# First norm of a hybrid S5 and conformer trunk: statistics asked for a block ahead, slabs loaded before the large S5 arrays, first block modulated like the others

## The chip, the cores and the metric

One core of one Trainium2 chip runs the whole program. The metric is the device time of one execution, in microseconds (us). All tensors are float32. The core has five engines that run their own instruction streams in order: TensorE (PE, the matmuls), VectorE (DVE), ScalarE (ACT), GpSimd (POOL) and SyncE (SP, which here only issues DMAs).

## The reference, cut to what matters

One trunk layer over 2048 latent tokens of width 1024, with 256 context tokens in front:

```python
mod_l = silu(c) @ ada_w + ada_b            # shift, scale, gate: 6 x 1024
mod_c = silu(c_ctx) @ ada_w + ada_b
nl = rmsnorm(x,   norm1_g) * (1 + sc1)  + sh1       # (2048, 1024)
nc = rmsnorm(ctx, norm1_g) * (1 + csc1) + csh1      # (256, 1024)
zl = nl @ w_in                             # columns: S5 input 512 | conformer 1024 | gates 2048
zc = nc @ w_in[:, :512]                    # S5 input of the context
ys = s5_mixer(zl[:, :512], zc)             # bidirectional scan, latents start from the context's state
ya = (gelu(ys) * sigmoid(gelu(ys) @ w_glu)) @ w_a
yb = conformer(zl[:, 512:1536]) @ w_b      # GLU, depthwise conv of width 31, LayerNorm, swish
h  = x + g1 * ((sigmoid(ga) * ya + sigmoid(gb) * yb) @ w_out)
h  = h + g2 * conv_ffn(modulate(rmsnorm(h, norm2_g), sh2, sc2))
out = rmsnorm(h, final_g)
```

An rmsnorm needs, for every token, the reciprocal root of its mean square. The kernel holds tokens along the free axis of a tile (channels on partitions), so this number is needed as a row that is the same in all partitions.

## The kernel before, in words

**Products.** Every large product is done in three passes (`mm3`, L462 to L464): both operands are split into a rounded part and a remainder, `hi` and `lo`, and hi by hi, hi by lo and lo by hi are summed in PSUM. The split of a weight chunk is a copy on ACT (L449) and a subtraction on POOL or, later, on DVE (L453).

**Modulation vectors** (`ada_first`). 2048 columns of `ada_w` come in 8 slabs of 1 MB (L574). Each slab feeds four matmuls (L577, 32 in all, two records each in the trace). The four sums are copied to `adarow`, two on DVE and two on ACT (L584), and 16 small transposes (L586) and two DVE operations (L591, L593) turn them into columns `A1` and `S1`. Between the slabs `after(k)` issues other work: pieces of the S5 parameters (`s5_params`, a generator), the statistics of the context and, at the end, of the first token block.

**Statistics** (`half_stats`, 256 tokens each). A load of the tokens (L619), two ACT squares with a running sum (L622), and `rstd`: five small DVE operations and a power on POOL (L476 to L482). `row` then makes the row: for each 128 tokens a diagonal matrix `dg` on DVE (L630) and a matmul with ones (L631), which leaves the row in PSUM.

**First norm.** The latents are worked in 4 blocks of 512 tokens, `nl0` to `nl3`, loaded transposed (L638, tiles `xt`). The context, `nlc`, has 256. The context and block 0 are normed in two steps: `early` multiplies by the row (L644, on DVE, it needs only the statistics) and `late` multiplies by `A1` and adds `S1` (L650), rounds on ACT (L652) and subtracts (L654). Blocks 1 to 3 go through `prepare` and `modulate`: row and `A1` in one DVE operation (L661), shift and rounding in one ACT operation (L662), remainder on DVE (L663).

**S5 input** (`pair`). Column tiles of 128 are done two at a time, each pair 48 matmuls: two pairs for the context (256 columns each matmul) and two for each block (512 columns). The result leaves PSUM by an ACT copy (L668) and two or one stores issued from ACT's queue (L671). Behind these stand the conformer products, whose tiles go through sigmoids on ACT (L840), the S5 tables (`s5_tables`: 32 groups, per group POOL L245, L246 and L249, DVE L247, L248 and L250, ACT L251 to L253, a store L254, three groups in a buffer of the pool `z8`), the S5 operators (`s5_ops`: POOL and DVE products, PE L308 and L318, stores L310 and L312 and later L328 to L330), and the depthwise conv (L795), whose input `caw` is loaded again from memory by SP (L784).

**What sets the order.** The program asks for work in the order of the Python code; a scheduler places each instruction in its engine's stream, with a head start of 300 for what stands in `urgent`. The streams are fixed before the program runs. Buffers come from small pools (`z8` 8, raw weights 3, `t16` 6, PSUM sums 4), so a load stands in its queue until its buffer is free, and all that is behind it in that queue stands too.

Of the kernel before, what the change touches and what calls it, by code (L numbers as in the profile page):

```python
# [19 lines left out]
CTX = 256  # L20
# [5 lines left out]
NCC = CTX // T  # L26
# [83 lines left out]
def s5_params(nc, ins, scr, st, sp, tp, ident, halfpi, psum):  # L110


    v, g_, a = nc.vector, nc.gpsimd, nc.scalar
    dma = nc.sync.dma_start
# [5 lines left out]
    dma(lm, ins["s5s"])  # L120
    lr, li, ldt = (lm[:, i, :] for i in range(3))
    bri = tp(128, 2, G, H)
    dma(bri, ins["s5b"])
    br, bi = bri[:, 0], bri[:, 1]
    cri = sp.big(128, 2, G, H)
    dma(cri, ins["s5c"])
    cr, ci = cri[:, 0], cri[:, 1]
    dn = sp(48, G)
    dma(dn[32:48, :], ins["s5d"])
    yield  # L130

    q, s = exp_parts(nc, tp, ldt, n)
# [4 lines left out]
    q, s = exp_parts(nc, tp, x, n)  # L137
# [11 lines left out]
    th, k, f = (tp(128, n) for nm in ("th", "kk", "f"))  # L149
# [71 lines left out]
    v.tensor_tensor(f8l, f8, f8h, op=OP.subtract)  # L221
    yield

    bbr, bbi = sp.big(128, G, H), sp.big(128, G, H)
    u1 = tp(128, G, H)
    u2 = tp(128, G, H)
# [204 lines left out]
class Net:  # L431
# [165 lines left out]
    def phase1(self):  # L597
        nc, tc, ins, scr, v, a = self.nc, self.tc, self.ins, self.scr, self.v, self.a
        w_in = ins["w_in"]
        with ExitStack() as ctx:  # L600
# [8 lines left out]
            self.consts()  # L609
            st = {}  # L610
            s5a = s5_params(nc, ins, scr, st, sp, tp, self.ident, self.halfpi, psum)
            nl, srow, xt = {}, {}, {}
            rms = small.tile([128, 18], F32, name="rms", bufs=1)

            def half_stats(i):

                x2 = self.z8("x2", [128, 2, D])
                src = ins["x"][256 * i:256 * i + 256, :] if i < 8 else ins["ctx"]
                self.dma(x2, src.rearrange("(j p) d -> p j d", p=128))  # L619
                ss = small.tile([128, 2], F32, name="nt_ss")  # L620
                for j in range(2):
                    a.activation(x2[:, j, :], x2[:, j, :], AF.Square, accum_out=ss[:, j:j + 1])  # L622
                self.rstd(small, ss, 2, 1.0 / D, rms[:, 2 * i:2 * i + 2])

            def row(i, n):

                ps = psum.tile([128, 512], F32, name="ps", tag="ax")
                for j in range(n // 128):
                    dg = small.tile([128, 128], F32, name="dg")
                    v.tensor_scalar(dg, self.ident, rms[:, 2 * i + j:2 * i + j + 1], None, op0=OP.mult)  # L630
                    self.pe.matmul(ps[:, 128 * j:128 * j + 128], self.ones, dg, start=True, stop=True)  # L631
                return ps

            def raw_block(b):

                for q in range(2):
                    t = self.z8("xt", [128, 4, 512])
                    self.dma(t, ins["xt"][b][:, 4 * q:4 * q + 4])  # L638
                    xt[b, q] = t

            def early(x, rs, n):

                for w in x:
                    v.tensor_tensor(w, w, rs[:, None, :].to_broadcast([128, 4, n]), op=OP.mult)  # L644

            def late(x, hi, lo, r):

                for k in range(8):
                    w = x(k)
                    v.tensor_scalar(w, w, self.A1[:, r, k:k + 1], self.S1[:, r, k:k + 1],  # L650
                                    op0=OP.mult, op1=OP.add)
                    a.copy(hi(k), w)  # L652
                    e = self.g if k % 4 == 3 else v
                    e.tensor_tensor(lo(k), w, hi(k).bitcast(F32), op=OP.subtract)  # L654

            def modulate(b):
                nl[b] = self.nl_tiles(b, "nl")
                for k in range(8):
                    hi, lo = nl[b](0, k), nl[b](1, k)
                    w, s1 = xt[b, k // 4][:, k % 4], self.S1[:, 0, k:k + 1]  # L660
                    v.scalar_tensor_tensor(w, w, self.A1[:, 0, k:k + 1], srow[b], op0=OP.mult, op1=OP.mult)  # L661
                    a.activation(hi, w, AF.Identity, bias=s1)  # L662
                    v.scalar_tensor_tensor(lo, w, s1, hi.bitcast(F32), op0=OP.add, op1=OP.subtract)  # L663
# [11 lines left out]
            def pair(ms, n, x, x0s):  # L675

                pss = [psum.tile([128, 512], F32, name="ps", tag="mm") for _ in ms]
                for k in range(8):
                    for ps, m in zip(pss, ms):
                        self.mm3(ps[:, :n], wu[m][k], x(k), k == 0, k == 7)  # L680
                for ps, m in zip(pss, ms):
                    u_out(ps, n, m, x0s)

            def u_block(b):
                for ms in ((0, 1), (2, 3)):
                    pair(ms, 512, lambda k: (nl[b](0, k), nl[b](1, k)), [NCC + 64 * b])

            xc = self.z8("xt", [128, 8, CTX])

            def after(k):  # L690
                if k == 0:
                    next(s5a)
                if k == 1:
                    self.dma(xc, ins["ctxt"])
                    half_stats(8)
                    early([xc[:, 4 * q:4 * q + 4] for q in range(2)], row(8, CTX)[:, :CTX], CTX)
                if k in (2, 3, 4, 5):
                    next(s5a, None)
                if k == 7:
                    for m in range(2):  # L700
                        wu[m] = self.wtile(ring, w_in, 128 * m)
                    raw_block(0)
                    for i in range(2):
                        half_stats(i)
                    early([xt[0, q] for q in range(2)], row(0, 512), 512)

            self.ada_first(psum, after)
            with self.urgent():
                late(lambda k: xc[:, k], lambda k: nlc(0, k), lambda k: nlc(1, k), 1)
            for m in range(2, 4):  # L710
                wu[m] = self.wtile(ring, w_in, 128 * m)
            nl[0] = self.nl_tiles(0, "nl")
            with self.urgent():
                late(lambda k: xt[0, k // 4][:, k % 4], lambda k: nl[0](0, k), lambda k: nl[0](1, k), 0)
            for ms in ((0, 1), (2, 3)):
                pair(ms, CTX, lambda k: (nlc(0, k), nlc(1, k)), [0, NX - NCC])
            self.low = "v"

            def prepare(b):
                raw_block(b)  # L720
                srow[b] = row(2 * b, 512)
                with self.urgent():
                    modulate(b)

            for i in (2, 3):
                half_stats(i)
            prepare(1)
            for i in (4, 5, 6, 7):
                half_stats(i)
            u_block(0)  # L730
            for _ in s5a:
                pass
            idx = sp(128, NX)
# [3 lines left out]
                        allow_small_or_imprecise_dtypes=True)  # L737
            tabs = s5_tables(nc, scr, st, idx, lambda: self.z8("tab", [128, 6 * NX]), self.halfpi)
            for b in range(1, 4):
                if b < 3:  # L740
                    prepare(b + 1)
                u_block(b)
                for _ in range((0, 3, 6, 9)[b]):
                    next(tabs, None)
            self.dma(self.fw, ins["fdw"])
            up.close()
# [665 lines left out]
```

## Time and profile before

| | |
|---|---|
| Time, 3 runs | 2806.5, 2810.7 and 2811.0 us; median 2810.7 us |
| Profiled execution | 2806.18 us, of which the span of the instructions 2804.4 us |
| PE busy | 2711.9 us, 97% of the span, 12044 matmul records |
| DVE, ACT, POOL busy | 1508.0 us (54%), 822.7 us (29%), 459.3 us (16%) |
| Mean granted TensorE clock | 0.984 of full speed |
| Chain that ended last | PE 75%, DVE 9%, DMA 6%, POOL 5%, issue 2%, ACT 2% |

The table is read so: with PE busy for 97% of the span, what is left to gain lies in the stretches in which PE waits, or runs at half its clock. The profile's page in 40 slices shows the first slice of 70 us with PE busy for 7 tenths and a clock of 8 tenths, the lowest of all. The change lies in the first three slices.

### The profile page before, as it was taken

How to read it: one execution, taken by the hardware profiler on the slowest of the kernel's cores; microseconds unless marked ns; L12 is line 12 of the kernel's file. 1: busy time of each engine (PE TensorE's matmuls, PEld its weight loads, DVE VectorE, ACT ScalarE, POOL GpSimd, SP SyncE). 2: the span in 40 equal slices, each digit the busy share in tenths (PEclk: the TensorE clock that was granted, in tenths of full speed). 3: DMA queues.
4: the chain of work that ended last, by engine and by line, in shares of the span. 5: the costliest groups of instructions: out<-in, count | busy, mean ns of one | idle time of the engine just before them, and what ended most of it. 6: DMA issues, size and time to landing. Idle time of an engine off the chain costs nothing.

```text
span 2804.4 us, 32119 instructions
## 1 busy us (share of the span) xinstructions
PE 2711.9 (97%) x12044; PEld 2203.2 (79%) x12044; DVE 1508.0 (54%) x2312; ACT 822.7 (29%) x1446; POOL 459.3 (16%) x504
## 2 busy tenths in 40 slices
PE   7998999999999999999999999999999989999998
PEld 3786878788887777788888888888888878787887
DVE  5867643433316788566855646556465462414154
ACT  2555412121235443243421222212222132212122
POOL 2256477667600000000000000000000000000000
PEclk8999999999999999999999999999999999999999
DMA  8645745354436576533111111111111153323143
GB/s 315 195 142 165 205 138 153 126 177 147 145 102 202 173 206 200 187 131 113 64 46 57 42 49 49 49 53 46 45 57 42 53 179 107 113 71 135 53 143 98
DMA packets 327308, 334.73 MB, mean 119 GB/s; under 512 B 95336, under 2 KB 240360, under 8 KB 324464
## 3 DMA queue, kind: packets, MB, share of 16 engines
q1 hardware_dynamic: 245680, 235.13, 27.2%
q10 hardware_dynamic: 81472, 97.54, 10.0%
q8 instruction: 95, 1.56, 0.2%
q14 instruction: 61, 0.50, 0.1%
HBM read 230.38 MB, written 102.21 MB: 119 GB/s over the span
## 4 chain that ended last, share of the span: by engine, by line
PE 75%; DVE 9%; DMA 6%; POOL 5%; issue 2%; ACT 2%; SPq 0%; ACTq 0%; POOLq 0%; DVEq 0%
PE ps L464 23%; PE ps L462 23%; PE ps L463 23%; DMA sgab<-d_sg 2%; PE ps L795 1%; DVE Hs L408 1%; PE ps L577 1%; PE ps L385 1%; POOL t L395 1%; DVE Hs L410 1%; DMA slab<-in_ada_w_dram 1%; DMA ada<-in_ada_w_dram 1%; POOL t L394 1%; POOL t L361 1%; PE ps L1112 0%
## 5 line engine op out<-in xcount | busy, mean ns | idle before, releaser
L1242 DVE SCALAR_TENSOR_TENSOR acc<-pad,fw,acc 128x1024 f32<-128x1024 f32 x352 | 450.4, 1282 | 238.9 <-ACT acc L1238 229.5
L477 POOL TENSOR_TENSOR rs_y<-rs_v,mhalf 128x1 f32<-128x1 f32 (+1 forms) x41 | 27.4, 668 | 2048.8 <-DVE rs_v L476 2048.8
L462 PE MATMUL ps<-wd,hhl 128*128 128x512 f32 x704 | 275.6, 393 | 13.5 <-ACT hhl L449 7.3
L463 PE MATMUL ps<-wd,hhl 128*128 128x512 f32 x704 | 275.7, 392 | 0.0
L464 PE MATMUL ps<-wd,hhl 128*128 128x512 f32 x704 | 275.3, 392 | 0.1
L408 DVE TENSOR_TENSOR_SCAN Hs<-m,S 64x287 f32<-64x287 f32 x64 | 68.8, 1075 | 240.5 <-POOL S L396 240.1
L453 DVE TENSOR_TENSOR hhl<-hr,hhl 128x512 fp32r<-128x512 f32 (+1 forms) x110 | 63.0, 582 | 244.4 <-ACT hhl L449 244.1
L453 DVE TENSOR_TENSOR w_ch<-w_raw,w_ch 128x512 fp32r<-128x512 f32 x134 | 106.4, 801 | 137.9 <-ACT w_ch L449 137.5
L462 PEld LDWEIGHTS ps<-wd,hhl 128*128 128x128 f32 x704 | 133.2, 189 | 43.3 <-ACT hhl L449 7.9
L449 ACT CAST w_ch<-w_raw 128x512 fp32r<-128x512 f32 x142 | 87.6, 621 | 267.2 <-PE ps L464 167.1
L463 PEld LDWEIGHTS ps<-wd,hhl 128*128 128x128 f32 x704 | 133.2, 189 | 28.6 <-DVE wd L453 1.0
L464 PEld LDWEIGHTS ps<-wd,hhl 128*128 128x128 f32 x704 | 133.1, 189 | 28.5 <-DVE hhl L453 0.8
L449 ACT CAST hhl<-hr 128x512 fp32r<-128x512 f32 (+1 forms) x110 | 57.2, 534 | 264.5 <-PE ps L464 231.3
L463 PE MATMUL ps<-nm2l,w_ch 128*128 128x512 f32 x344 | 133.8, 389 | 0.0
L464 PE MATMUL ps<-nm2h,w_ch 128*128 128x512 f32 x344 | 133.8, 389 | 0.0
L462 PE MATMUL ps<-nm0h,w_ch 128*128 128x512 f32 x344 | 133.8, 389 | 0.0
L463 PE MATMUL ps<-nm0l,w_ch 128*128 128x512 f32 x344 | 133.8, 389 | 0.0
L463 PE MATMUL ps<-nm1l,w_ch 128*128 128x512 f32 x344 | 133.8, 389 | 0.0
L463 PE MATMUL ps<-nm3l,w_ch 128*128 128x512 f32 x344 | 133.8, 389 | 0.0
L464 PE MATMUL ps<-nm0h,w_ch 128*128 128x512 f32 x344 | 133.8, 389 | 0.0
L462 PE MATMUL ps<-nm1h,w_ch 128*128 128x512 f32 x344 | 133.8, 389 | 0.0
L464 PE MATMUL ps<-nm1h,w_ch 128*128 128x512 f32 x344 | 133.8, 389 | 0.0
(370 smaller groups left out, 6354.5 us busy)
## 6 DMA issues: line engine op xcount, KB each, us to landing
w_raw<-in_ffn_w_up_dram SPq DMA_DIRECT2D x88, 256.0 KB
d_hid<-acc ACTq DMA_DIRECT2D x88, 256.0 KB
w_raw<-in_ffn_w_down_dram SPq DMA_DIRECT2D x76, 256.0 KB
grp<-d_rec SPq DMA_DIRECT2D x32, 576.0 KB
hr<-d_hid SPq DMA_DIRECT2D x66, 256.0 KB
d_sg<-sgg ACTq DMA_DIRECT2D x64, 256.0 KB
ada<-in_ada_w_dram SPq DMA_DIRECT2D x64, 256.0 KB
sgab<-d_sg SPq DMA_DIRECT2D x32, 512.0 KB
```

Of the source, the lines that this page charges most:

```text
L361: g_.tensor_tensor(r1, Hl, tb[:, 0:1, LAT].to_broadcast([128, 2, NCL]), op=OP.mult)
L385: nc.tensor.matmul(ps[:, :NX], sm[:, i, :], ug, start=True, stop=True)
L394: g_.tensor_tensor(t1, S, tb[:, 0:1, :].to_broadcast([128, 2, NX]), op=OP.mult)
L395: g_.tensor_tensor(t2, S[:, ::-1, :], tb[:, 1:2, :].to_broadcast([128, 2, NX]), op=OP.mult)
L408: v.tensor_tensor_scan(Hs[0:64, i, 1:1 + nsc], mb[0:64], S[0:64, i, 0:nsc], 0.0, op0=OP.mult, op1=OP.add)
L410: v.tensor_tensor_scan(Hs[64:128, i, NX - 1 - nsc:NX - 1][:, ::-1], mb[64:128], S[64:128, i, NX - nsc:NX][:, ::-1], 0.0, op0=OP.mult, op1= ...
L449: self.a.copy(hi, src)
L453: e.tensor_tensor(lo, src, hi.bitcast(F32), op=OP.subtract)
L462: mm(ps, wh, xh, start=first, stop=False)
L463: mm(ps, wh, xl, start=False, stop=False)
L464: mm(ps, wl, xh, start=False, stop=last)
L1242: v.scalar_tensor_tensor(acc[:, h], win(h, t // 3, t % 3), fw[:, i, t:t + 1], acc[:, h], op0=OP.mult, op1=OP.add)
```

## The change

The order of loading changes: in `s5_params` the three loads of the larger S5 arrays (`s5b`, `s5c`, `s5d`) stand behind the parameter work instead of before the second slab. In `after` the context is loaded and its statistics are made behind slab 5 instead of slab 1, its row and its `early` step at slab 7, the S5 pieces at 2, 3, 4 and 6 instead of 2 to 5, and at slab 7 block 0's statistics stand ahead of its transposed load. Block 0 loses `early` and `late` and goes through `prepare(0)`. `prepare(b)` asks for block b's row and modulation and then for the loads and statistics of block b+1; it stands between the two column pairs of the block before. Tables are asked for after each pair, 27 of 32 ahead of the conformer products instead of 18.

```diff
@@ s5_params
     bri = tp(128, 2, G, H)
-    dma(bri, ins["s5b"])
...
     cri = sp.big(128, 2, G, H)
-    dma(cri, ins["s5c"])
...
     dn = sp(48, G)
-    dma(dn[32:48, :], ins["s5d"])
     yield
...
+    dma(bri, ins["s5b"])
+    dma(cri, ins["s5c"])
+    dma(dn[32:48, :], ins["s5d"])
     bbr, bbi = sp.big(128, G, H), sp.big(128, G, H)
@@ phase1
-            def u_block(b):
-                for ms in ((0, 1), (2, 3)):
-                    pair(ms, 512, lambda k: (nl[b](0, k), nl[b](1, k)), [NCC + 64 * b])
+            def u_block(b, h):
+                pair((2 * h, 2 * h + 1), 512, lambda k: (nl[b](0, k), nl[b](1, k)), [NCC + 64 * b])
...
-                if k == 1:
+                if k == 5:
+                    half_stats(8)
                     self.dma(xc, ins["ctxt"])
-                    half_stats(8)
-                    early([xc[:, 4 * q:4 * q + 4] for q in range(2)], row(8, CTX)[:, :CTX], CTX)
-                if k in (2, 3, 4, 5):
+                if k in (2, 3, 4, 6):
                     next(s5a, None)
                 if k == 7:
+                    early([xc[:, 4 * q:4 * q + 4] for q in range(2)], row(8, CTX)[:, :CTX], CTX)
                     for m in range(2):
                         wu[m] = self.wtile(ring, w_in, 128 * m)
-                    raw_block(0)
                     for i in range(2):
                         half_stats(i)
-                    early([xt[0, q] for q in range(2)], row(0, 512), 512)
+                    raw_block(0)
...
-            nl[0] = self.nl_tiles(0, "nl")
-            with self.urgent():
-                late(lambda k: xt[0, k // 4][:, k % 4], lambda k: nl[0](0, k), lambda k: nl[0](1, k), 0)
-            for ms in ((0, 1), (2, 3)):
+
+            def u_ctx(ms):
                 pair(ms, CTX, lambda k: (nlc(0, k), nlc(1, k)), [0, NX - NCC])
-            self.low = "v"
 
             def prepare(b):
-                raw_block(b)
+
                 srow[b] = row(2 * b, 512)
                 with self.urgent():
                     modulate(b)
-
-            for i in (2, 3):
-                half_stats(i)
+                if b < 3:
+                    for i in (2 * b + 2, 2 * b + 3):
+                        half_stats(i)
+                    raw_block(b + 1)
+
+            u_ctx((0, 1))
+            prepare(0)
+            u_ctx((2, 3))
+            self.low = "v"
+            u_block(0, 0)
             prepare(1)
-            for i in (4, 5, 6, 7):
-                half_stats(i)
-            u_block(0)
+            u_block(0, 1)
...
             for b in range(1, 4):
+                u_block(b, 0)
                 if b < 3:
                     prepare(b + 1)
-                u_block(b)
-                for _ in range((0, 3, 6, 9)[b]):
+                for _ in range((0, 3, 6, 6)[b]):
+                    next(tabs, None)
+                u_block(b, 1)
+                for _ in range((0, 3, 3, 6)[b]):
                     next(tabs, None)
```

Three places in the streams, before and after. The first is SP's queue from the first slab on. `slab` is `ada_w`, `ctxt` the transposed context (2048 columns, 1 MB), `x_139` and `x_227` the context for its statistics, `x_316` and `x_330` the first tokens for theirs. Before:

```order
L574 DMA slab<-in_ada_w_dram 128x2048
L120 DMA tp_95<-in_s5s_dram 128x96
L123 DMA tp_95<-in_s5b_dram 128x1024
L126 DMA sp_96<-in_s5c_dram 128x1024
L129 DMA sp_97<-in_s5d_dram 16x32
L574 DMA slab<-in_ada_w_dram 128x2048
L694 DMA xt<-in_ctxt_dram 128x2048
L619 DMA x_139<-in_ctx_dram 128x2x1024
L574 DMA slab<-in_ada_w_dram 128x2048 x6
L496 DMA w_raw<-in_w_in_dram 128x4x128 x3
L638 DMA xt<-in_xt_dram 128x2048
L496 DMA w_raw<-in_w_in_dram 128x4x128
```

And after:

```order
L574 DMA slab<-in_ada_w_dram 128x2048
L120 DMA tp_95<-in_s5s_dram 128x96
L574 DMA slab<-in_ada_w_dram 128x2048 x5
L619 DMA x_227<-in_ctx_dram 128x2x1024
L694 DMA xt<-in_ctxt_dram 128x2048
L574 DMA slab<-in_ada_w_dram 128x2048 x2
L496 DMA w_raw<-in_w_in_dram 128x4x128 x3
L619 DMA x_316<-in_x_dram 128x2x1024
L496 DMA w_raw<-in_w_in_dram 128x4x128
L619 DMA x_330<-in_x_dram 128x2x1024
L638 DMA xt<-in_xt_dram 128x2048 x2
```

Six slabs now stand ahead of the context, the S5 arrays are gone from here (they stand behind the transposed load of block 2), and block 0's tokens stand ahead of its transposed tiles.

The second is PE's stream from its first matmul to the first one of the context's products. Before:

```order
L577 MATMUL ps<-slab,sc 2x512 x32
L631 MATMUL ps<-dg,ones 128x128 x3
L586 MATMUL ps<-ident,adarow 128x2 x16
L631 MATMUL ps<-dg,ones 128x128
L462 MATMUL ps<-nlch,w_ch 128x256 x3
```

And after:

```order
L577 MATMUL ps<-slab,sc 2x512 x24
L631 MATMUL ps<-dg,ones 128x128 x2
L577 MATMUL ps<-slab,sc 2x512 x8
L586 MATMUL ps<-ident,adarow 128x2 x4
L631 MATMUL ps<-dg,ones 128x128
L586 MATMUL ps<-ident,adarow 128x2 x8
L631 MATMUL ps<-dg,ones 128x128
L586 MATMUL ps<-ident,adarow 128x2 x4
L631 MATMUL ps<-dg,ones 128x128 x2
L462 MATMUL ps<-nlch,w_ch 128x256 x2
```

The context's row is made between slabs 5 and 6, and all four parts of block 0's row stand ahead of the first product of the context. Before, two of them were there, and the other two stood within the context's products.

The third is ACT's stream where the conformer products begin, with the first casts of their weights (L449). Before:

```order
L254 DMA d_rec<-tab 128x640
L668 COPY ub<-ps 128x512
L449 CAST w_ch<-w_raw 128x512 x2
L671 DMA d_u<-ub 1024x1x64
L668 COPY ub<-ps 128x512
L449 CAST w_ch<-w_raw 128x512
L671 DMA d_u<-ub 1024x1x64
L252 ACTIVATE tab<-tab 128x320
```

And after:

```order
L251 ACTIVATE tab<-tab 128x320
L254 DMA d_rec<-tab 128x640
L449 CAST w_ch<-w_raw 128x512 x2
L252 ACTIVATE tab<-tab 128x320
L253 ACTIVATE tab<-tab,halfpi 128x320
L668 COPY ub<-ps 128x512
L254 DMA d_rec<-tab 128x640
L671 DMA d_u<-ub 1024x1x64
L668 COPY ub<-ps 128x512
L251 ACTIVATE tab<-tab 128x320
L671 DMA d_u<-ub 1024x1x64
```

The copies that free PSUM (L668) stood next to the casts and stand behind a table's operations now, and two more of them, which came before the casts earlier, follow 27 rows further down behind 6 more tables.

## Rows read from the trace of the kernel before

**Rows 1.** PE's timeline up to the context's products; start, length, work, [idle before <-releaser]

```profile
6.40 8.68 PE L577 MATMUL ps<-slab,sc 128*2 128x512 f32 x16 [6.40 <-DMA slab<-in_ada_w_dram]
19.22 22.46 PE L577 MATMUL ps<-slab,sc 128*2 128x512 f32 x48 [4.15 <-DMA slab<-in_ada_w_dram]
...
47.93 0.80 PE L631 MATMUL ps<-dg,ones 128*128 128x128 f32 x2 [5.60 <-DVE dg L630]
48.66 1.86 PE L586 MATMUL ps<-ident,adarow 2*128 2x2 f32 x16
...
51.95 1.01 PE L462 MATMUL ps<-nlch,w_ch 128*128 128x256 f32 x3 [0.71 <-ACT nlch L652]
```

**Rows 2.** Windows: stretch, length, busy PE, PEld, DVE, ACT, POOL, PEclk, DMA, GB/s

```profile
20.00:22.00 2.00, 2.00 (x3) 0.26 (x2) 1.93 (x12) 0.00 (x0) 0.00 (x0) 0.50 1.01 426
22.00:24.00 2.00, 2.00 (x5) 0.38 (x4) 1.22 (x8) 0.00 (x0) 0.49 (x1) 0.76 1.01 426
...
50.00:60.00 10.00, 8.52 (x36) 7.40 (x37) 8.44 (x17) 6.40 (x15) 6.33 (x6) 0.50 0.47 159
...
80.00:90.00 10.00, 9.71 (x40) 8.01 (x41) 6.04 (x16) 6.11 (x12) 0.69 (x1) 0.83 1.02 371
...
100.00:110.00 10.00, 7.43 (x29) 5.67 (x28) 8.10 (x29) 2.61 (x6) 2.44 (x3) 0.83 0.72 236
...
240.00:260.00 20.00, 13.41 (x55) 11.47 (x56) 17.36 (x30) 12.18 (x23) 14.99 (x23) 0.74 0.47 152
```

**Rows 3.** ACT's timeline: squares of block 0's tokens, stores of the context's S5 input

```profile
45.38 0.19 ACT L622 ACTIVATION_READ_ACCUMULATOR x<-x 128x1 f32 x1
45.95 1.06 ACT L622 ACTIVATE x<-x 128x1024 f32<-128x1024 f32 x1 [0.38 <-DVE adarow L584]
...
64.71 4.97 ACTq L671 DMA_DIRECT2D d_u<-ub  x3
```

**Rows 4.** DVE's timeline: diagonals, row step of block 0, block 1's modulation

```profile
47.59 1.50 DVE L630 TENSOR_SCALAR dg<-ident,rms 128x128 f32<-128x128 f32 x2
...
62.29 4.48 DVE L644 TENSOR_TENSOR xt<-xt,ps 128x2048 f32<-128x2048 f32 x2 [0.61 <-PE ps L631]
...
85.60 2.73 DVE L661 SCALAR_TENSOR_TENSOR xt<-xt,mod,ps 128x512 f32<-128x512 f32 x4 [2.88 <-PE ps L631]
```

**Rows 5.** PE's timeline: context's products, then the blocks', to the first conformer product

```profile
57.34 0.41 PE L463 MATMUL ps<-nlcl,w_ch 128*128 128x256 f32 x1
...
60.11 0.41 PE L464 MATMUL ps<-nlch,w_ch 128*128 128x256 f32 x1
...
62.32 0.28 PE L462 MATMUL ps<-nlch,w_ch 128*128 128x256 f32 x1
...
69.39 0.28 PE L464 MATMUL ps<-nlch,w_ch 128*128 128x256 f32 x1
70.39 0.50 PE L462 MATMUL ps<-nl0h,w_ch 128*128 128x512 f32 x1 [0.72 <-ACT nl0h L652]
...
71.69 0.39 PE L462 MATMUL ps<-nl0h,w_ch 128*128 128x512 f32 x1
...
75.09 0.39 PE L462 MATMUL ps<-nl0h,w_ch 128*128 128x512 f32 x1
...
80.29 0.71 PE L631 MATMUL ps<-dg,ones 128*128 128x128 f32 x4 [2.88 <-DVE dg L630]
...
103.08 0.49 PE L631 MATMUL ps<-dg,ones 128*128 128x128 f32 x2 [2.08 <-DVE dg L630]
...
171.92 0.50 PE L462 MATMUL ps<-nl0h,w_ch 128*128 128x512 f32 x1 [0.71 <-ACT w_ch L449]
```

**Rows 6.** PE's timeline: the two longest waits in the conformer products

```profile
246.59 2.90 PE L795 MATMUL ps<-caw,ctw 128*128 128x128 f32 x12 [7.32 <-ACT tab L253]
...
263.74 0.50 PE L462 MATMUL ps<-nl0h,w_ch 128*128 128x512 f32 x1 [2.26 <-ACT w_ch L449]
```

**Rows 7.** POOL's timeline: a table that waits for its buffer

```profile
201.54 1.04 POOL L245 TENSOR_SCALAR tab<-sp 128x320 f32<-128x320 f32 x2 [15.32 <-DMA d_rec<-tab]
```

## The prediction

> **What bounds the kernel now.** I read the page's busy times first, then the windows of the first 300 us, then PE's timeline there, and last the engines that PE's gaps name. PE is busy for 97% of the span, so a change that keeps the number of large matmuls can only win or lose in PE's gaps and in stretches at half clock. Both are dense at the start. PE waits 4.15 us for the third slab [rows 1]; the windows right behind show a granted clock of 0.50 and 0.76 [rows 2]. It then waits 5.60 us for a diagonal of block 0's statistics, while the 16 transposes of the modulation stand behind that diagonal in its stream [rows 1], and the clock is 0.50 from 50 to 60 us. 2.88 and 2.08 us more go to diagonals of later blocks [rows 5], with a mean clock of 0.83 in both those windows [rows 2]. After that PE has no gap until the last S5 input product, and the first conformer product starts at 171.92 us. In the conformer stretch it waits 7.32 and 2.26 us [rows 6].
>
> I follow three marks: the first product of the context (51.95 us), the first of block 0 (70.39 us) and the first conformer product (171.92 us).
>
> **Part 1, to the context's first product.** What ends this stretch before is not the modulation alone but the second half of block 0's statistics: its squares begin at 45.95 us [rows 3], and the diagonals and the transposes follow. In SP's queue three things leave the place ahead of that load: both transposed tiles of block 0 (128 by 2048 floats, 1.05 MB each) and the two large S5 arrays (0.52 MB each), 3.15 MB together. The windows around 20 us moved 426 GB/s with all DMA engines busy [rows 2], so 3.15 MB are 7.4 us, and the squares begin at about 45.95 - 7.4 = 38.6 us. The slabs are no longer the limit: six of them stand ahead of the context, and PE needs over 3 us for one (22.46 us for six) [rows 1], while one lands every 1.05 / 0.426 = 2.5 us. So the 4.15 us wait goes, and with it the half clock behind it, worth 2 x 0.50 + 2 x 0.24 = 1.5 us. PE ends the slabs at 41.68 - 4.15 - 1.5 = 36.0 us, ahead of the statistics; these 5.7 us are therefore worth nothing by themselves, and the statistics are what is late next.
>
> From the start of those squares it takes two squares (1.06 us each, the second overlapping a little) [rows 3]; then come, side by side, rms and diagonal (2.0 us before, from the first half's sum at 45.57 to the diagonal at 47.59) [rows 3, 4] with the last matmuls of the row, and the adarow copies with the transposes and the first step of the context (3.3 us from the first transpose at 48.66 to the first product at 51.95) [rows 1]. 38.6 + 2.1 + 3.3 = 44.0 us. The first product starts 8 us earlier. Bounds: 41.5 us if the load also gains the time that SP spends between the loads before, 47 us if it stands behind the fourth weight chunk's buffer.
>
> Rule against it: the Trainium skill, "DMA: Bandwidth & Descriptors", section Specifications, gives a limit of about 358 GB/s for the memory per core. By that figure the 13.7 MB that stand ahead of or in the second statistics load would take 38 us instead of 32, and the first product would start some 6 us later than in my sum. The windows here show 426 GB/s, so I keep the row's figure.
>
> **Part 2, the context's products.** Before, 96 matmuls take 18.4 us (51.95 to 70.39). At half clock they come every 0.213 us (13 steps between 57.34 and 60.11), at full clock every 0.120 us (59 steps between 62.32 and 69.39) [rows 5]. PE idles between the slabs' end at 36 and the first product at 44, so the low clock stays for some 9 us: 43 x 0.213 + 53 x 0.120 = 15.5 us at least. Block 0's `early` step goes (4.48 us), and its 8 first DVE operations at 0.68 us (2.73 / 4) [rows 4], with 8 for the remainder that I put at the same, take 10.9 us beside these matmuls. The row for them is there before the context starts. Against that, casts of the last weight chunks and block 0's roundings stand among the context's copies and stores on ACT, whose store issue held ACT for 4.97 us before [rows 3]. Bounds 15.5 and 22 us; I take 18.4 us as before, since the cast and the store are the nearest row to what is late next. Block 0 begins at 62.4 us.
>
> **Part 3, the four blocks.** 384 matmuls at 0.227 us (15 steps between 71.69 and 75.09) [rows 5] are 87.1 us, the rows of blocks 1 to 3 some 2 us: 89 us. They took 100.8 us (70.39 to 171.2), so 11.8 us are lost before: 2.88 and 2.08 us of waits, 2 x 1.7 us of low clock [rows 2, 5], and small ones. In the new order the statistics stand a block ahead, and a row is asked for between the two pairs, 48 matmuls (10.9 us) before the block that needs it. DVE needs 10.9 us for a block (16 x 0.68), just what PE needs for a pair; so the modulation has no slack within the pair and small waits remain. Bounds: 0 lost, and all 11.8 us again. I take 5, so 94 us, and the conformer products begin at about 157 us, 15 us earlier than before.
>
> **Part 4, the conformer stretch.** Nothing is taken out here, but two things are moved. 27 tables are asked for ahead of it instead of 18, and PE reaches it 15 us earlier; so POOL, DVE and ACT have more to do in less time ahead of it, and less within it. Before, this stretch loses 0.71, 7.32 and 2.26 us, and its low clock (0.74 of 20 us, PE busy for 13.4) [rows 2, 5, 6] about 3.5 us, 13.8 in all. The 7.32 us stand under a table, but the matmuls also need `caw`, which SP loads behind stores of operators that POOL makes; I hold that for the cause. In the new order five more such stores stand ahead of those loads, but PE also has more small S5 matmuls ahead of them. On ACT the copies that free PSUM for the first conformer products stand behind table operations now. Each such place can wait for POOL and DVE to make a table. I count four such places and a wait of 7.32 us at most in a row of this kind [rows 6]; at 3 us each (my estimate, under half of that row) they are 12 us, with some 2 us of low clock behind them 14. That is what the stretch loses before. So I take nothing, with a range of 10 us to the good (4 left) and 15 us to the bad, below.
>
> Later stages keep their instructions. Sum: -8 (part 1), 0, -7 (part 3, 101 to 94), 0 = -15 us; 2806.2 - 15 = 2791.2 us. The profiled execution lies 4.5 us under the median of the runs shown and at their lower end; I put the forecast at 2792.
>
> **Rivals.**
> (a) The conformer stretch gains too, since nine tables fewer are asked for within it and sigmoids meet fewer of them: 4 us lost instead of 14, so 2781 us. For it speaks that POOL stood idle for 15.32 us at the beginning of that stretch [rows 7], so that work could be done earlier; against it, that this idle time was a wait for a table's buffer.
> (b) A table's buffer takes the gain back. ACT runs in order. The two tables ahead of a PSUM copy wait for a buffer as POOL did, 15.32 us [rows 7], PE's sums stay full and PE stands. Once is 15.3 us: 2806.5 us, no change.
> (c) Slower: the same mechanism twice, once in the roundings of block 2 or 3 (table operations stand among them on ACT now) and once at the conformer's beginning: -15 + 2 x 15.3 = +15.6, 2822 us. It decides from the second such wait on. For it: less time for 27 tables. Against: before, PE had no gap while 18 tables were made.
> (d) The first part does not do what it says, because the statistics' load lands no earlier (SP waits for a weight buffer ahead of it): only part 3 gains, 7 us, 2799 us.
>
> **How the numbers follow.** A measurement of this kernel can tell about 0.2%, 5.6 us, from no change. Forecast 0.45; (a) 0.18; (d) 0.10; (b) 0.14; (c) 0.13. Faster: 0.45 + 0.18, 0.09 of (d) and 0.04 of (b) = 0.76. Same: 0.11, most of (b). Slower: 0.13. Range 2775 to 2809 us: the lower end is (a) with part 2 at its lower bound and 3 us more in part 3, the upper takes in (d) and (b); (c) is left out. The likeliest case's own range is 2783 to 2800.
>
> **What would show it.** Part 1: no wait for a slab, and the first product of the context near 44 us. Part 2: block 0's first product near 62 us. Part 3: waits for diagonals below 1 us each, the first conformer product near 157 us. Part 4: ACT's copies of the last S5 inputs late behind tables, a wait of the first `caw` matmuls for SP. The prediction is wrong if the load of block 0's second half lands after 42 us, or if PE stands for more than 10 us in one place between block 1 and the first conv.

## The result: slower by 0.8%, and the profile after

| | before | after |
|---|---|---|
| Median | 2810.7 us | 2832.9 us |
| Profiled execution, span | 2804.4 us | 2828.1 us |
| Ratio to before, 95% interval | | 1.0078, 1.0062 to 1.0094 |
| PE busy | 2711.9 us | 2715.9 us |

The forecast was 2792 us with a range of 2775 to 2809; the time lies above it. PE's timeline of the kernel after, with the marks of the prediction and every wait above 2 us behind the context's first product, up to 250 us (start, length, work, idle time before it and who ended it; the later lines carry numbers higher by 3):

```profile
43.99 0.80 PE L462 MATMUL ps<-nlch,w_ch 128*128 128x256 f32 x2
...
58.75 0.40 PE L462 MATMUL ps<-nl0h,w_ch 128*128 128x512 f32 x1
...
75.54 0.50 PE L462 MATMUL ps<-nl0h,w_ch 128*128 128x512 f32 x1 [3.92 <-ACT ub L668]
...
105.69 1.22 PE L631 MATMUL ps<-dg,ones 128*128 128x128 f32 x4 [6.47 <-DVE dg L630]
...
166.31 0.50 PE L462 MATMUL ps<-nl0h,w_ch 128*128 128x512 f32 x1 [2.52 <-ACT ub L668]
...
170.00 0.80 PE L464 MATMUL ps<-nl0h,w_ch 128*128 128x512 f32 x1 [2.95 <-DVE w_ch L453]
...
188.47 0.64 PE L462 MATMUL ps<-nl2h,w_ch 128*128 128x512 f32 x1 [4.97 <-ACT ub L668]
...
205.34 0.50 PE L462 MATMUL ps<-nl0h,w_ch 128*128 128x512 f32 x1 [4.12 <-ACT av L843]
...
228.90 0.90 PE L308 MATMUL ps<-ident,ab 128*128 128x128 f32 x3 [5.28 <-DVE ab L281]
...
248.22 1.68 PE L318 MATMUL ps<-ca,sp 128*48 128x144 f32 x6 [3.96 <-DVE ca L296]
```

The reader is to see three marks and where the waits lie. The context's first product starts at 43.99 us (before 51.95 [rows 1]), block 0's at 58.75 us (before 70.39), the conformer's at 166.31 us (before 171.92 [rows 5]). So the lead over the kernel before is 8.0, 11.6 and then only 5.6 us. The last six waits, 23.8 us together, stand where before had 0.71, 7.32 and 2.26 us [rows 5, 6]. The last sigmoid of the gates made beside the S5 stage ends this stretch: it starts at 891.5 us before and at 911.6 us after, 20.1 us late. From there to the end of the span it is 1912.9 and 1916.5 us. The lead of 5.6 us has turned into a lag of 20.1 between these two marks, 25.7 us; the rest of the program adds 3.6. That last figure is small beside what profiles of one stretch differ by: in the ten runs below with 15 or more tables asked for ahead, the part behind the last gate takes 1917.4 to 1922.9 us, and the 1912.9 of before is the shortest of all.

The windows of the kernel after, columns as in [rows 2]:

```profile
76.00:80.00 4.00, 4.00 (x13) 3.08 (x12) 0.00 (x0) 2.01 (x4) 0.00 (x0) 0.57 0.96 143
...
106.00:110.00 4.00, 4.00 (x12) 3.32 (x12) 3.99 (x7) 2.39 (x5) 0.84 (x2) 0.50 0.22 50
...
150.00:200.00 50.00, 39.56 (x157) 31.54 (x156) 41.76 (x68) 24.62 (x55) 39.33 (x58) 0.90 0.54 163
200.00:250.00 50.00, 36.60 (x159) 27.59 (x158) 33.14 (x62) 26.64 (x75) 24.54 (x34) 0.86 0.30 101
```

and the same 100 us of the kernel before:

```profile
150.00:200.00 50.00, 49.29 (x217) 40.37 (x216) 29.24 (x53) 32.12 (x63) 26.21 (x39) 1.00 0.57 164
200.00:250.00 50.00, 42.68 (x204) 34.91 (x203) 39.42 (x66) 22.00 (x55) 36.23 (x54) 0.91 0.38 131
```

Between 150 and 250 us PE idles for 23.8 us after and 8.0 us before. The lower clock costs busy time times the missing share: 39.56 x 0.10 + 36.60 x 0.14 = 9.1 us after, 42.68 x 0.09 = 3.8 before. The whole stretch from the first conformer product to the last of these sigmoids gives the 25.7 us exactly. After, then before:

```profile
166.31:911.60 745.29, 703.98 (x3239) 574.67 (x3240) 312.56 (x497) 216.51 (x477) 384.32 (x380) 0.97 0.48 147
```

```profile
171.92:891.50 719.58, 693.74 (x3235) 567.42 (x3236) 315.54 (x498) 229.71 (x492) 380.90 (x380) 0.99 0.50 153
```

PE idles for 41.3 us after and 25.8 before, 15.5 more, and nearly the same number of matmuls keeps it busy for 10.2 us longer, at a mean granted clock of 0.97 against 0.99. DVE and POOL are busy for 83% and 79% of the first 50 us after, against 58% and 52%: the tables have moved into the stretch in which the conformer products begin.

Who holds PE's copies and sigmoids there is seen in ACT's timeline of the kernel after:

```profile
75.11 0.37 ACT L668 COPY ub<-ps 128x256 f32<-128x256 f32 x1 [11.03 <-DMA d_u<-ub]
...
183.35 0.47 ACT L251 ACTIVATE tab<-tab 128x320 f32<-128x320 f32 x1 [7.23 <-DVE tab L250]
...
186.88 0.55 ACT L253 ACTIVATE tab<-tab,halfpi 128x320 f32<-128x320 f32 x1
187.33 0.60 ACT L449 CAST w_ch<-w_raw 128x512 fp32r<-128x512 f32 x1
...
187.84 1.06 ACT L668 COPY ub<-ps 128x512 f32<-128x512 f32 x2
...
203.40 1.28 ACT L843 ACT_TABLE_LOAD   x1 [0.81 <-DMA d_rec<-tab]
204.69 2.06 ACT L843 ACTIVATE av<-ps 128x512 f32<-128x512 f32 x4
```

The wait of 11.03 us lies earlier and comes back under Part 3. At 183 us ACT stands for 7.23 us in front of a table that DVE hasn't made. The two copies of the last S5 inputs, whose sums PE had finished before 164 us, run at 187.84 us behind three such tables, and PE, whose PSUM buffers are full, goes on at 188.47. The first sigmoids run at 204.69 us, all four at once; before they began at 186.0. In ACT's stream they stand behind 25 tables, before behind 16. ACT is not alone: three of the six waits, 12.2 us, were ended by DVE (`w_ch` at L453, `ab` at L281, `ca` at L296), on whose stream the tables' own operations stand too.

### The profile page after: what moved, and what is told of

Read it like the earlier page. It is cut to its first block, busy times and chain, and to the rows that moved or that the text cites. A ratio compares the mean times of both kernels' runs of the same rounds, so it can differ in the third digit from the quotient of the medians.

```text
span 2828.1 us, 32126 instructions
## 1 busy us (share of the span) xinstructions
PE 2715.9 (96%) x12044; PEld 2205.0 (78%) x12044; DVE 1501.6 (53%) x2312; ACT 812.3 (29%) x1438; POOL 457.0 (16%) x502
## 4 chain that ended last, share of the span: by engine, by line
PE 69%; DVE 10%; DMA 8%; POOL 7%; issue 4%; ACT 3%; SPq 0%; ACTq 0%; POOLq 0%; DVEq 0%
PE ps L464 22%; PE ps L462 22%; PE ps L463 22%; DMA sgab<-d_sg 2%; DVE Hs L408 1%; POOL t L395 1%; PE ps L798 1%; DVE Hs L410 1%; DMA ada<-in_ada_w_dram 1%; DMA d_u<-ub 1%; POOL t L394 1%; DMA w_raw<-in_w_in_dram 1%; POOL t L361 1%; POOL S L396 1%; POOL t L362 1%
## 5 line engine op out<-in xcount | busy, mean ns | idle before, releaser
L477 POOL TENSOR_TENSOR rs_y<-rs_v,mhalf 128x1 f32<-128x1 f32 (+1 forms) x41 | 25.7, 626 | 2093.2 <-DVE rs_v L476 2093.1
L453 DVE TENSOR_TENSOR hhl<-hr,hhl 128x512 fp32r<-128x512 f32 (+1 forms) x110 | 63.0, 582 | 243.0 <-ACT hhl L449 242.8
L453 DVE TENSOR_TENSOR w_ch<-w_raw,w_ch 128x512 fp32r<-128x512 f32 x134 | 104.0, 782 | 137.9 <-ACT w_ch L449 137.6
L449 ACT CAST w_ch<-w_raw 128x512 fp32r<-128x512 f32 x142 | 87.7, 621 | 254.0 <-PE ps L464 166.8
L464 PE MATMUL ps<-nm2h,w_ch 128*128 128x512 f32 x344 | 133.8, 389 | 0.0
L462 PE MATMUL ps<-nm2h,w_ch 128*128 128x512 f32 x344 | 133.8, 389 | 0.0
L462 PE MATMUL ps<-nm3h,w_ch 128*128 128x512 f32 x344 | 133.8, 389 | 0.0
```

The source lines that it names most:

```text
L449: self.a.copy(hi, src)
L453: e.tensor_tensor(lo, src, hi.bitcast(F32), op=OP.subtract)
L462: mm(ps, wh, xh, start=first, stop=False)
L464: mm(ps, wl, xh, start=False, stop=last)
```

## The experiments

Theory T: the number of tables asked for ahead of the conformer products costs the time. Theory D: the loads a block ahead do. Each ratio is to the kernel before, run beside it on the same chip. That kernel's median was 2810.7 us beside the change and 2815, 2812 and 2814 us beside the three groups of variants, so ratios are compared, not times.

| kernel | tables ahead | ratio, 95% interval |
|---|---|---|
| after | 27 | 1.0078, 1.0062 to 1.0094 |
| `tab18` | 18 | 0.9981, 0.9970 to 0.9992 |
| `before_tab27` | 27 | 1.0085, 1.0062 to 1.0108 |
| `ubc` | 27 | 1.0077, 1.0057 to 1.0097 |
| `after_cheap` | 27 | 1.0004, 0.9993 to 1.0015 |
| `prologue` | 18 | 0.9958, 0.9945 to 0.9972 |
| `prologue_again` | 18 | 0.9965, 0.9954 to 0.9977 |
| `mod0` | 18 | 0.9975, 0.9962 to 0.9987 |
| `tab18_late` | 18 | 0.9988, 0.9979 to 0.9998 |
| `prologue_tab21` | 21 | 0.9984, 0.9972 to 0.9995 |
| `prologue_tab15` | 15 | 1.0016, 1.0006 to 1.0026 |
| `prologue_tab9` | 9 | 1.0043, 1.0029 to 1.0057 |
| `tab9` | 9 | 1.0048, 1.0030 to 1.0067 |

**`tab18`.** The change with the old numbers of tables.

```diff
-                for _ in range((0, 3, 6, 6)[b]):
+                for _ in range((0, 0, 0, 0)[b]):
                     next(tabs, None)
                 u_block(b, 1)
-                for _ in range((0, 3, 3, 6)[b]):
+                for _ in range((0, 3, 6, 9)[b]):
```

> The changed kernel with the S5 tables asked for as in the kernel before: none between two column pairs, 0, 3, 6 and 9 after a block, 18 ahead of the conformer products instead of 27. Everything else as changed. Theory T (the tables: the nine more stand on ACT, POOL and DVE ahead of the casts, PSUM copies and sigmoids with which the conformer products begin, and PE waits there, 23.8 us in six waits between 166 and 248 us): most of these waits go, 2833 falls by 18 to 26 us to about 2810, and the sigmoids of the first four sums come behind 15 tables, not 25. Theory D (the loads a block ahead: they fill the DMA queues, the stores of the S5 input come late, ACT stands and all that follows is late): the time stays within 6 us of 2833.

Measured 0.9981: 1.0078 to 0.9981 is some 27 us. (`ubc`, which has the change's 27 tables, ran beside `tab18` and gave 1.0077.) PE's timeline of `tab18` where the six waits were:

```profile
162.32 0.50 PE L462 MATMUL ps<-nl0h,w_ch 128*128 128x512 f32 x1 [0.87 <-ACT w_ch L449]
...
168.00 0.80 PE L464 MATMUL ps<-nl0h,w_ch 128*128 128x512 f32 x1 [4.25 <-DVE w_ch L453]
...
246.36 2.90 PE L798 MATMUL ps<-caw,ctw 128*128 128x128 f32 x12 [9.48 <-DMA caw<-d_av]
```

The waits for ACT's copies and sigmoids are gone. The wait for `caw` is back. Before it stood under the name of a table [rows 6]; here the trace names the load. Theory D is out as the main cause.

**`before_tab27`.** The other direction: the kernel before, 27 tables.

```diff
-                for _ in range((0, 3, 6, 9)[b]):
+                for _ in range((0, 6, 9, 12)[b]):
```

> The kernel before with 6, 9 and 12 tables after blocks 1 to 3, so 27 ahead of the conformer products instead of 18, nothing else changed. Theory T: slower than before by 12 to 25 us (2823 to 2836), with waits of PE for ACT's copies and sigmoids between 170 and 250 us. Theory D: within 6 us of 2810.7.

Measured 1.0085, as slow as the whole change. PE's timeline of `before_tab27`:

```profile
212.12 0.80 PE L462 MATMUL ps<-nl0h,w_ch 128*128 128x512 f32 x1 [10.57 <-ACT av L840]
...
234.37 0.90 PE L308 MATMUL ps<-ident,ab 128*128 128x128 f32 x3 [5.76 <-ACT tab L253]
```

There is one wait of 10.57 us for the first sigmoids and one of 5.76 us for the operators. The number of tables alone makes a loss of this size, without anything else of the change.

**`after_cheap`.** The order untouched, each table cheaper to make. L246 and L249, two of POOL's three operations for a table, are left out and the sines' scale is made small, so the tables hold other numbers.

```diff
         g_.tensor_scalar(tk, idx, h, MAGIC, op0=OP.mult, op1=OP.add)
-        g_.tensor_scalar(tk, tk, -MAGIC, 1.0, op0=OP.add, op1=OP.mult)
...
-        g_.tensor_scalar(tk, tt, 1.0, MAGIC, op0=OP.mult, op1=OP.add)
...
-        a.activation(tt, tt, AF.Sin, scale=-6.283185)
-        a.activation(tk, tk, AF.Sin, scale=-6.283185, bias=halfpi)
+        a.activation(tt, tt, AF.Sin, scale=-1e-9)
+        a.activation(tk, tk, AF.Sin, scale=-1e-9, bias=halfpi)
```

> The changed kernel, order and number of tables untouched (27 asked for ahead), but each table is made cheaper on POOL: two of its three POOL operations (L246, L249) are left out, so that the tables hold other numbers. Theory T2 (a backlog: of 27 tables asked for only some 14 are made when the conformer products begin, since each takes POOL and DVE in turn, and the casts, copies and sigmoids stand on ACT behind the rest): with the tables made sooner the waits of PE between 163 and 250 us shrink from 23.8 us to under 10, and the time falls by 10 to 25 us below 2833. Theory P (it is the order on ACT and ACT's own 1.5 us per table, not the making on POOL and DVE): less than 6 us below 2833.

Measured 1.0004, 0.74% or 21 us below the change. PE's timeline of `after_cheap` (lines lower by 2):

```profile
160.71 0.50 PE L460 MATMUL ps<-nl0h,w_ch 128*128 128x512 f32 x1 [2.52 <-ACT ub L666]
...
174.52 0.50 PE L460 MATMUL ps<-nl2h,w_ch 128*128 128x512 f32 x1 [2.19 <-ACT ub L666]
...
190.70 0.80 PE L460 MATMUL ps<-nl0h,w_ch 128*128 128x512 f32 x1 [5.01 <-ACT av L841]
...
213.59 0.81 PE L306 MATMUL ps<-ident,ab 128*128 128x128 f32 x3 [3.52 <-DVE ab L279]
...
235.35 0.50 PE L462 MATMUL ps<-nl0h,w_ch 128*128 128x512 f32 x1 [2.24 <-DVE w_ch L451]
```

The waits have much the same places, 15.5 us instead of 23.8 (I had expected under 10), and the first sigmoids run at 190.05 us, 14.6 earlier. When the conformer products begin, 15 tables have been sent to memory in both kernels, and 10 more stand ahead of the first sigmoids. From the first conformer product to these sigmoids it is 29 us here and 38 in the change. So it is a backlog: how long a table takes to make, times the tables that stand ahead and aren't made. The order alone does not set the price. Two things stay mixed: 5.6 us were gained before the conformer products began (160.71 against 166.31), and the lighter POOL helps everything else that POOL does there.

**`prologue`, `prologue_again`.** The kernel before with the loading order alone: the part of the diff in `s5_params` and in `after(k)`, block 0 keeping `early` and `late`.

> The kernel before with only the order of loading of the change: slabs ahead of the large S5 arrays, the context behind slab 5, block 0's statistics ahead of its transposed tiles. Block 0 keeps its two steps, statistics and tables stay as before. Theory T and D both: the context's first product starts near 44 us instead of 52, and if nothing further down takes it back the time is 5 to 8 us below before, 2803 to 2806. If the gain is absorbed by the next wait (weight chunks, tables that can't run earlier), it is 2808 to 2811.

> The loading order of the change alone once more, beside the two with other numbers of tables: 2800 to 2806, below before by 0.2 to 0.5%.

Measured 0.9958 and 0.9965, faster than both kernels. PE's timeline of `prologue`:

```profile
43.14 0.79 PE L462 MATMUL ps<-nlch,w_ch 128*128 128x256 f32 x2 [1.64 <-ACT nlch L652]
...
81.50 1.23 PE L631 MATMUL ps<-dg,ones 128*128 128x128 f32 x4 [8.38 <-DVE dg L630]
...
166.78 0.50 PE L462 MATMUL ps<-nl0h,w_ch 128*128 128x512 f32 x1 [0.71 <-ACT w_ch L449]
...
243.60 2.90 PE L795 MATMUL ps<-caw,ctw 128*128 128x128 f32 x12 [8.87 <-ACT tab L251]
```

The first product leads by 8.8 us. At the first conformer product 5.1 us of that are left, behind a wait of 8.38 us for a diagonal. `prologue_again` is the same kernel, and its profile shows how far two executions differ: that wait is 6.04 us, the first conformer product starts at 161.45 us, 10.5 us ahead of before, and the last gate sigmoid at 880.4 us, where `prologue` has 886.5 and before 891.5. So behind the blocks a mark of one profile does not tell differences below some 6 us. The two ratios are a gain of 10 to 12 us. That is about the lead at block 0's first product, 12.0 and 12.5 us, since the context's products are 3 us shorter too.

**`ubc`.** The change with a buffer of its own for the context's last S5 input tile.

```diff
-                ub = rp.tile([128, T, 64], F32, name="ub", tag="ub", bufs=2)
+                if n == CTX and m == 3:
+                    ub = rp.tile([128, T, 32], F32, name="ubc", tag="ubc", bufs=1)
+                else:
+                    ub = rp.tile([128, T, 64], F32, name="ub", tag="ub", bufs=2)
```

> The changed kernel with a buffer of its own for the last S5 input tile of the context, so that ACT's copy of it doesn't wait for a store to land (11.03 us of ACT at 64 to 75 us, with a wait of PE of 3.92 us and half clock behind it). Theory D: 5 to 12 us faster than the changed kernel, since what stood behind that copy on ACT moves up. Theory T: 0 to 5 us faster, and the waits after 163 us stay.

Measured 1.0077, no change. PE's timeline of `ubc`:

```profile
102.65 1.22 PE L631 MATMUL ps<-dg,ones 128*128 128x128 f32 x4 [8.31 <-DVE dg L630]
...
163.48 0.50 PE L462 MATMUL ps<-nl0h,w_ch 128*128 128x512 f32 x1 [2.52 <-ACT ub L671]
```

ACT's 11.03 us and PE's 3.92 us behind it are gone, the next wait grew from 6.47 to 8.31 us, and the conformer begins 2.8 us earlier. The last gate sigmoid still starts 2.8 us earlier (908.8 against 911.6), but nothing of that is seen in the time. It is less than two profiles of one kernel differ by.

**`mod0` and `tab18_late`.** `mod0` is `prologue` with block 0 through `modulate` (the lines below leave out the loading order); `tab18_late` is `tab18` with the next block's loads and statistics asked for behind the second pair.

```diff
-                    early([xt[0, q] for q in range(2)], row(0, 512), 512)
...
-            nl[0] = self.nl_tiles(0, "nl")
+            srow[0] = row(0, 512)
             with self.urgent():
-                late(lambda k: xt[0, k // 4][:, k % 4], lambda k: nl[0](0, k), lambda k: nl[0](1, k), 0)
+                modulate(0)
```

> The kernel before with the loading order of the change, and block 0 put through row, L661, L662 and L663 as the others; statistics, rows and tables as before (18). If the first block's modulation is what costs the changed order its advantage over the loading order alone: 2806 to 2812. If it is neutral, 2799 to 2804; if it gains (4.48 us of DVE removed ahead of block 0's products), 2795 to 2800.

> The changed kernel with 18 tables, and the loads and statistics of the next block asked for behind the second column pair of the block before it, not between the pairs; rows stay between the pairs. Theory O (on DVE and POOL the statistics of the block after next stand ahead of the diagonals of the next block, and PE waits 4.0 us for a diagonal at 100 us with half clock behind): that wait goes, 4 to 7 us below 2809. Theory B (what ends the u blocks early is lost again at the beginning of the conformer products, whose weights and tables don't come earlier): within 3 us of 2809.

`mod0` 0.9975, `tab18_late` 0.9988. The intervals of `mod0` and the two runs of `prologue` overlap, so the first block's modulation is worth nothing that these runs can tell. In `tab18_late` the wait at 104 us fell from 4.03 to 1.09 us, but another of 9.61 us came at 80 us, behind later statistics; the time did not fall. That is the time of theory B, but not a test of it: the blocks did not end earlier (first conformer product at 162.83 us against 162.32), so nothing was there to be lost again.

**`prologue_tab9`, `tab9`, `prologue_tab15`, `prologue_tab21`.** Other numbers of tables: (0, 3, 3, 3), (0, 3, 6, 6) and (0, 3, 6, 12) after the blocks.

> The kernel before with the loading order of the change alone, and with 3 tables after each of blocks 1 to 3, 9 ahead of the conformer products instead of 18. Theory T (each table ahead of the conformer products delays ACT's copies, casts and sigmoids there; nine more cost 24 to 27 us): fewer cost less, below the 2802 us of the loading order with 18, by 3 to 15 us. Theory S (18 is the point up to which the engines have room; below it nothing is to be had, and the nine tables come back between the conformer products): within 3 us of 2802, or above it.

> The changed kernel with 9 tables ahead of the conformer products instead of 27. Theory T: below the 2809 us of the changed kernel with 18, by 3 to 15 us. Theory S: within 3 us of 2809 or above.

> The loading order of the change alone with 3, 6 and 6 tables after blocks 1 to 3, 15 ahead instead of 18. Theory T2: little or no backlog at the beginning of the conformer products either way, so within 5 us of the 2802 us with 18. If the time rises steadily from 18 down to 9 (2802 to 2825): about 2809.

> The loading order of the change alone with 3, 6 and 12 tables, 21 ahead. Theory T2: three more tables stand in the backlog, each some 2.5 us of waits: 2806 to 2814. If only the sigmoids' place counts (behind 18 tables instead of 16): within 5 us of 2802.

Fewer is worse too: 1.0043 and 1.0048 at 9, 1.0016 at 15. That theory T, read as "each table ahead costs", is wrong below 18. Theory S holds, as far as it went: it left open how much slower 9 would be. With 15 the time was to be within 5 us of that with 18 by theory T2, and 2809 us on a steady rise; it was 2818.8 us, 14.8 above `prologue_again` beside it, so neither fits and two thirds of the rise lie between 18 and 15. With 21 it was 2809.1 us, 5.1 above `prologue_again`. That lies in the 2806 to 2814 of theory T2, at the edge of what can be told. The S5 scans of `prologue`, then of `prologue_tab9` (count, shortest, median and longest in ns, first and last start):

```profile
L408 DVE TENSOR_TENSOR_SCAN Hs<-m,S x64: 747/1070/1414, 348.2 to 750.6; 64x287 f32<-64x287 f32 x64
```

```profile
L408 DVE TENSOR_TENSOR_SCAN Hs<-m,S x64: 747/1068/1416, 360.8 to 771.7; 64x287 f32<-64x287 f32 x64
```

With 9 ahead all 9 tables have been sent to memory when the conformer products begin, at 161 us and with a wait of only 0.27 us, but the last S5 scan starts 21 us later. The last gate sigmoid is at 887.8 us, and in the two profiles of the loading order with 18 at 886.5 and 880.4; what follows takes 1932 us against 1919 and 1923, and `tab9` against `tab18` shows the same (1934 and 1920). So most of the time is lost behind that sigmoid. With 15 it is lost ahead of it: the sigmoid is at 897.5 us, 11 and 17 us later, and what follows takes 1922. PE waits there for 10.1 us on a POOL operation of the S5 stage (L363; 2.9 in `prologue_again`) and for 12.3 on remainders of weights (7.9). Why too few tables ahead cost what they do was not tried further and stays open.

## Why the prediction was wrong

In the terms of the sum, measured on the profiled executions: part 1 gave -8.0 us (forecast -8), part 2 -3.7 (forecast 0), part 3 +4.2 (forecast -7), part 4 up to the last gate sigmoid +27.5 (forecast 0), and the later stages +3.6 (forecast 0). Together that is +23.7 where the forecast had -15.

**Part 1 held.** First product at 43.99 us, forecast 44.0. The second squares began at 37.89 us, forecast 38.6, and no slab was waited for after the first. That the mark fits to 0.01 us is luck: the squares came 0.7 us sooner, and the chain behind them took 6.1 us instead of 5.4. The limit of 358 GB/s in the Trainium skill ("DMA: Bandwidth & Descriptors", Specifications) would have put that load some 6 us later, by the estimate in the prediction. The window from 36 to 40 us moved 432 GB/s, and the measurement decides:

```profile
36.00:40.00 4.00, 1.17 (x3) 0.09 (x1) 1.99 (x9) 3.13 (x7) 1.97 (x2) 1.00 1.03 432
```

**Part 2 was better than forecast.** 14.8 us from the context's first product to block 0's, where I took 18.4. This is below my lower bound of 15.5, since the low clock lasted for some 5 us, not 9: the matmuls start every 0.213 us until 48.5 us and every 0.120 us behind that. `prologue` and `prologue_again`, which keep block 0's two steps, took 15.3 and 15.1 us, so nearly all of this comes with the loading order.

**Part 3 failed in size and sign.** I took 94 us for the four blocks ("I take 5" lost); they took 105.0 (58.75 to 163.79), 4 us more than before. Nor is this one profile: in all six kernels that ask for statistics a block ahead they took 100.0 to 105.0 us, where before took 100.8. The two waits of 3.92 and 6.47 us are larger than those that went (2.88 and 2.08), and the clock behind them was 0.57 and 0.50. (Of the low clock before, the second window of [rows 2] gives 7.43 x 0.17 = 1.3 us, not the 1.7 that I wrote for both; this changes little.) What I had not priced is what the requests a block ahead stand in front of. The context's stores share the DMA engines with loads of the next block, and ACT waited 11.03 us for one to land. On DVE the statistics of block 3 stand ahead of the second pair of diagonals of block 2. The timeline of DVE in the kernel after:

```profile
102.54 0.41 DVE L478 TENSOR_TENSOR rs_z<-rs_y 128x2 f32<-128x2 f32 x1 [1.09 <-POOL rs_y L477]
...
105.08 0.15 DVE L482 TENSOR_TENSOR rms<-rs_y,rs_z 128x2 f32<-128x2 f32 x1
105.15 0.67 DVE L630 TENSOR_SCALAR dg<-ident,rms 128x128 f32<-128x128 f32 x2
```

`ubc` and `tab18_late` show that taking one of these waits away brings another, and neither moved the time. `tab18` (0.9981) has all of the change but the tables, and `prologue` (0.9958 and 0.9965) only its loading order. So the rest of the change gained nothing; it may have cost some 0.2%, which is at the edge of what these intervals tell.

**Part 4 is the step that made the result.** "I count four such places", "at 3 us each", and "That is what the stretch loses before. So I take nothing". The kind of place was right: copies, a weight's remainder, sigmoids and S5 operators all waited. The price was not. I had 12 us of waits and 2 us of low clock; there were 23.8 us in six waits and 9 us of low clock, and the stretch, for which I took no change, became 27.5 us longer. `tab18` gives that back, `before_tab27` makes a loss of this size alone, and `after_cheap` gives 21 us back with the order untouched. I priced each place as a wait for one table, but the engines run in order and their streams were laid out as if the tables were ready. Of the 27 tables asked for only 15 had been sent to memory when the first conformer product started, where before 12 of 18 had, so 12 were outstanding instead of 6. Each short operation for PE waits for as many tables as stand ahead of it and aren't made.

Neither of the two signs that I had named for a wrong prediction came: the second half of block 0's tokens had landed by 37.89 us, and PE never stood for 10 us in one place, at most for 6.47. The loss was spread over several waits, for which I had named no such sign.

**The rivals.** (c) came nearest: tables in front of work for PE cost more than 15 us. Its 2822 us was 11 us short, and its mechanism was another. It had ACT wait for a table's buffer, as POOL did in [rows 7], once among the roundings of a block and once at the conformer's beginning. But between 110 and 262 us POOL waited for table buffers for 0.5 us in all in the kernel after, against 17.1 before; the tables waited to be made, and ACT for them at the conformer's beginning. I gave (c) 0.13, because PE had no gap before while 18 tables were made. That said nothing on 27. (a), (b) and (d) did not occur.

## What to carry to other kernels

Background work asked for ahead of a stage delays that stage by what is not made when it begins, and an in-order engine passes the backlog on to its shortest instructions. Count how many pieces the engines have finished when the stage begins, and price what is left by the time that one piece takes. Asking only for what can be finished was not best here either: 9 tables were all made in time, and the kernel was slower than with 18, of which 12 were. The number has an optimum, 18 among the five tried, and it has to be looked for by runs. When a change has several parts, price the part that only renumbers something as carefully as the part that it is named after.

## What the runs showed that I had not expected

A store of 128 KB in short rows issued by ACT at 59.33 us had not landed by 75 us (ACT's next copy into that buffer starts at 75.11), while the DMA engines were busy with loads. Between 55 and 80 us, 7677 of the 8773 packets belonged to ACT's queue and carried 0.97 of 6.95 MB. The optimum in the number of tables was not expected either. With the new loading order 9, 15, 18 and 21 tables gave 1.0043, 1.0016, 0.9958 and 0.9965, and 0.9984; 27 gave 1.0085 with the old one.
